# Layer 0 of a hybrid decoder step with the second chunk of tokens reversed, and one product per HGRN level

## Chip, cores and metric

One NeuronCore of a Trainium2 chip runs the whole step. The metric is device time in microseconds (us) of one execution. Engines are named as the profile names them: PE (TensorE, the matrix multiplier), PEld (its weight loads), DVE (VectorE), ACT (ScalarE), POOL (GpSimd) and SP (the queue that issues the weight DMAs).

## The reference, cut to what matters

The program takes 256 prompt tokens and 8 sample tokens (264 columns) through two trunk layers. Layer 0 projects the tokens once and feeds two groups of heads in parallel: 4 retention heads of width 256 and 8 HGRN2 heads of width 128. The change concerns the HGRN2 heads, and the retention heads where they share the order of the tokens:

```python
def _hgrn2(q, k, v, log_f, s0):          # k = 1 - f, with f the forget gate
    def step(s, inp):
        qc, kc, vc, gc = inp
        b = jnp.cumsum(gc, axis=1)
        o_cross = jnp.einsum('bihd,bhdv->bihv', qc * jnp.exp(b), s)
        rel = jnp.exp(jnp.where(causal, b[:, :, None] - b[:, None, :], -jnp.inf))
        att = jnp.einsum('bihd,bjhd,bijhd->bhij', qc, kc, rel)
        o = o_cross + jnp.einsum('bhij,bjhv->bihv', att, vc)
        ...
# retention: the same, with one fixed decay per head
# then: out projection, residual add, a SwiGLU FFN, layer 1 (S5), a second FFN, a final norm
```

So the score of query i and key j is a sum over 128 channels, where each channel has its own decay: the product of the forget gates from j to i.

## The kernel before, in words

**Storage.** Activations lie feature-major: 128 features on the partitions, 264 tokens along the free axis (0 to 255 the prompt, 256 to 263 the samples).

**The stream.** All large products run as one stream of units (`Step.stream`, L104 to L143). A unit is 8 blocks of 128x128 weights. ACT rounds the weights to a high part `whi` (`split`, L85 to L96, the copy on L89), DVE subtracts for the low part `wlo` (L96; POOL does it for every eighth unit). PE then makes three products per block with 264 columns: high by high (L128), high weights by the low activations (L129), low weights by high (L131). `ahead` keeps four units split ahead, so the split of a later unit is emitted at the start of the present one; `flush` emits what was put off in `S.later`, right behind that split.

**Work of the heads.** After each unit `slot` lets the generators in `S.active` go one step. In layer 0 that is `mixers`: in each call it advances the sample generator (`hg_sample` or `ret_sample`: the recurrent states of the 8 sample tokens), then the tails of finished heads, then one of the heads in work (two HGRN heads in turn, or one retention head). The order of each engine's instructions is the order in which these lines are emitted; no scheduler moves them.

**An HGRN head** (`hg_head`, L453). Tokens form two chunks of 128. Inside a chunk a causal pair (i, j) is found at the level l of the highest bit in which the two positions differ: j lies in the left half of a block of 2^(l+1) tokens and i in the right half. For l = 0 to 6 the head does one step:

- PE multiplies, for each chunk j, all 128 keys by the 64 queries that stand in right halves (L496, fp32, two products of 64 columns);
- `decay(l + 1)` on DVE multiplies the left keys `hk` by the decay of the right half (L470) and the right queries `hq` by that of the left half (L471), and forms the next level's decays `pw` (L474);
- DVE copies the wanted scores from PSUM into `score` under a mask (L499).

Then come the product of chunk 1's queries with chunk 0's keys (L505, one product of 128 columns), the products with v (L512 to L515) and the tail.

**A retention head** (`ret_head`, L347): transposes (L355, L358), scores `p` (L360, L362), the decay mask `am` in two DVE products (L370, L371), the products with v (L376, L377), and a tail.

**Samples.** `hg_sample` rescales the states on ACT (L434), adds the outer products on DVE (L435), four states a step, and reads them on PE (L442). `ret_sample` does the same with L319, L322 and L327. `qz` (L280) holds the sample queries, `se` and `so` carry the result out (L285, L290, L293). `hg_sample` waits for the entry "qs", which the head sets in its first step.

**Leaving the layer.** `out_first` (L764) adds the residual column block by block; the RMS norm's sum is closed by the product of L225.

Of the kernel before, what the change touches and what calls it, by code (L numbers as in the profile page):

```python
# [28 lines left out]
C_MASK, C_KDEC, C_W = 0, 7 * 64, 7 * 64 + 8  # L29
# [211 lines left out]
def layer0(S, I, O):  # L241
# [105 lines left out]
    def ret_head(h, H):  # L347
        dec = S.st("pd", 1, w=256)
# [20 lines left out]
        am = S.st("am", 1, w=512)  # L369
        V.tensor_mul(am[:, :256], p[:, :256], dec)  # L370
        V.tensor_mul(am[:, 256:384], p[:, 256:384], dec[:, :128])  # L371
# [83 lines left out]
    def hg_head(h, H):  # L455
# [4 lines left out]
        halves = lambda x, l: x[:, :NP].rearrange("p (b t s) -> p b t s", t=2, s=1 << l)  # L460
        sc = score[h % 2]
        pw = S.st("pw", 2, w=256)
        P = {0: f[:, :NP]}

        def decay(l):

            Pv = P[l - 1].rearrange("p (b t) -> p b t", t=2)
            bc = lambda t: Pv[:, :, t:t + 1].to_broadcast([128, NP >> l, 1 << (l - 1)])
# [5 lines left out]
            V.tensor_mul(P[l], Pv[:, :, 0], Pv[:, :, 1])  # L474
# [11 lines left out]
        vt = S.st("vt", 2, w=256)  # L486
        acopy(vt, pvv[:, :256])
        yield
        at = 256
        for l in range(8):  # L490
            if l in (2, 6):
                pa, at = S.pt("a", 2), 0
            if l < 7:
                for j in range(2):
                    sl = slice(128 * j, 128 * j + 128)
                    PE.matmul(pa[:, at + 64 * j:at + 64 * j + 64], k[:, sl],  # L496
                              q[:, sl].rearrange("p (b t s) -> p b t s", t=2, s=1 << l)[:, :, 1, :], start=True, stop=True)
                decay(l + 1)
                V.copy_predicated(sc.rearrange("p j (b t s) -> p j b t s", t=2, s=1 << l)[:, :, :, 1, :],  # L499
                                  mask[:, C_MASK + 64 * l:C_MASK + 64 * l + 64].rearrange(  # L500
                                      "p (o b s) -> p o b s", o=1, s=1 << l).to_broadcast([128, 2, 64 >> l, 1 << l]),
# [217 lines left out]
    def mixers():  # L719
# [1039 lines left out]
def host(inputs):  # L1759
# [4 lines left out]
    xT = np.concatenate([xp, xs], 0).T[perm]  # L1764
# [16 lines left out]
    for l in range(7):  # L1781
        right = t[t >> l & 1 == 1]
        c[:, C_MASK + 64 * l:C_MASK + 64 * l + 64] = (t[:, None] >> l == (right[None] >> l) - 1)
    lg = np.log((1.0 - 2.0 ** (-5.0 - np.arange(RH))).astype(np.float32)).astype(np.float32).astype(np.float64)
    for h in range(RH):
        for j in range(2):
            c[:, C_KDEC + 2 * h + j] = np.exp((255 - 128 * j - t) * lg[h]) / 16
    A["cst"] = c
    i, j = np.arange(256)[None], t[:, None]
    A["rdec"] = np.stack([np.where(i >= j, np.exp((i - j) * lg[h]) / 16, 0.0) for h in range(RH)]).astype(np.float32)  # L1790
    inv = (10000.0 ** (-(t.astype(np.float32) / np.float32(128)).astype(np.float64))).astype(np.float32)
    pos = np.concatenate([np.arange(256), np.full(8, 2048)]).astype(np.float32)
# [49 lines left out]
```

## Time and profile before

| | us |
|---|---|
| device time, median of 3 runs | 2398.79 (2398.37 to 2399.08) |
| the profiled execution, device time | 2398.75 |
| the profiled execution, span on the core | 2396.9 |
| PE busy in the span | 2358.3 |
| DVE busy | 1600.3 |
| ACT busy | 1115.9 |
| POOL busy | 267.3 |
| mean granted TensorE clock | 0.996 |

The span runs from the first to the last instruction; 1.85 us of the device time lie around it. Layer 0's projection and heads take the span from 0 to about 480 us, the out projection follows to about 570, then come the first FFN, the S5 layer and the second FFN. An engine's busy time is an average over all of this. In the timeline a row gives start, length, engine, line, operation, tiles and the number of merged instructions. Ends of matmuls are modelled, so what a PE instruction costs is read from the starts of its neighbours. An fp32 product shows as two PE records, one for each pass over the weights.

### The profile page before, as it was taken

Reading aid. Unit: us, or ns where it says so; the run is one execution under the profiler, and the core shown is the slowest. Engines: PE = TensorE matmul, PEld = TensorE weight load, DVE = VectorE, ACT = ScalarE, POOL = GpSimd, SP = SyncE. Lnnn points to the kernel's source line nnn. Section 1 sums busy time; section 2 is a strip of 40 time slices with the busy share of each in tenths; the row PEclk is TensorE's granted clock in tenths of the full one; section 3 lists DMA queues with packets and bytes.
Section 4 is the critical chain, followed back from the end, with each engine's and each line's share of the span. In section 5 each row is a group of like instructions: output and inputs, shape, how many; then the busy total and the mean of one; then the engine's idle time right before and its main releaser. Section 6 shows DMA issues by size and latency. Waiting matters only on the chain.

```text
span 2396.9 us, 49380 instructions
## 1 busy us (share of the span) xinstructions
PE 2358.3 (98%) x20331; PEld 2324.7 (97%) x20331; DVE 1600.3 (67%) x2567; ACT 1115.9 (47%) x1612; POOL 267.3 (11%) x363
## 2 busy tenths in 40 slices
PE   8999999999999999999999989999999999999997
PEld 8999999999999999999999969999999999999997
DVE  6777777777877778877756685555555555555555
ACT  6464645554444344444444465454443344434444
POOL 3121111221020111012011140001000000000000
PEclk9999999999999999999999999999999999999999
DMA  7757566765557767777676885556556555565554
GB/s 240 244 201 246 207 234 220 245 209 189 184 195 225 231 218 235 225 224 229 218 239 181 311 316 185 176 186 207 179 182 180 184 184 180 183 182 180 183 165 136
DMA packets 189553, 499.58 MB, mean 208 GB/s; under 512 B 19408, under 2 KB 72128, under 8 KB 188816
## 3 DMA queue, kind: packets, MB, share of 16 engines
q1 hardware_dynamic: 176368, 452.83, 58.2%
q0 software_dynamic: 12960, 43.59, 5.5%
q8 instruction: 160, 2.62, 0.4%
q14 instruction: 65, 0.53, 0.1%
HBM read 452.44 MB, written 43.91 MB: 207 GB/s over the span
## 4 chain that ended last, share of the span: by engine, by line
PE 91%; DVE 3%; ACT 2%; DMA 2%; issue 1%; SPq 0%; DVEq 0%; ACTq 0%
PE acc L128 28%; PE acc L129 28%; PE acc L131 28%; ACT whi L89 1%; PE pa L496 1%; DVE wlo L96 1%; PE pt L1039 1%; DMA raw<-w_in 1%; DVE st L435 0%; DMA a2l<-wb 0%; DMA whi<-wb 0%; PE pt L1024 0%; PE ps L327 0%; PE pt L386 0%; PE pa L131 0%
## 5 line engine op out<-in xcount | busy, mean ns | idle before, releaser
L96 DVE TENSOR_TENSOR wlo<-raw,whi 128x1024 fp32r<-128x1024 f32 (+1 forms) x743 | 898.9, 1213 | 486.6 <-ACT whi L89 473.8
L89 ACT ACTIVATE whi<-raw 128x1024 fp32r<-128x1024 f32 (+1 forms) x767 | 794.0, 1040 | 840.7 <-PE acc L129 558.0
L128 PE MATMUL acc<-xh,whi 128*128 128x264 f32 x3776 | 1086.6, 288 | 7.4 <-ACT whi L650 7.4
L131 PE MATMUL acc<-xh,wlo 128*128 128x264 f32 x3776 | 1071.4, 284 | 0.0
L129 PE MATMUL acc<-xl,whi 128*128 128x264 f32 x3776 | 1070.3, 283 | 0.0
L128 PEld LDWEIGHTS acc<-xh,whi 128*128 128x128 f32 x3776 | 712.3, 189 | 10.9 <-ACT whi L650 7.7
L129 PEld LDWEIGHTS acc<-xl,whi 128*128 128x128 f32 x3776 | 713.3, 189 | 0.4
L131 PEld LDWEIGHTS acc<-xh,wlo 128*128 128x128 f32 x3776 | 709.2, 188 | 0.6 <-POOL wlo L651 0.6
L128 PE MATMUL acc<-a2h,whi 128*128 128x264 f32 x2080 | 594.3, 286 | 0.0
L131 PE MATMUL acc<-a2h,wlo 128*128 128x264 f32 x2080 | 590.0, 284 | 0.0
L129 PE MATMUL acc<-a2l,whi 128*128 128x264 f32 x2080 | 589.6, 283 | 0.0
L128 PEld LDWEIGHTS acc<-a2h,whi 128*128 128x128 f32 x2080 | 392.3, 189 | 1.8 <-issue 1.6
L129 PEld LDWEIGHTS acc<-a2l,whi 128*128 128x128 f32 x2080 | 392.5, 189 | 0.0
L131 PEld LDWEIGHTS acc<-a2h,wlo 128*128 128x128 f32 x2080 | 390.5, 188 | 0.1
L1754 POOL TENSOR_TENSOR xh<-xh,R 128x528 f32<-128x528 f32 x2 | 2.9, 1467 | 725.7 <-DVE R L189 725.7
L96 POOL TENSOR_TENSOR wlo<-raw,whi 128x1024 fp32r<-128x1024 f32 x24 | 58.1, 2423 | 155.0 <-ACT whi L89 141.6
L1589 DVE TENSOR_TENSOR x<-x,acc 128x264 f32<-128x264 f32 x96 | 41.1, 429 | 50.2 <-PE acc L131 49.9
L1577 DVE TENSOR_TENSOR up<-acc,R 128x264 f32<-128x264 f32 x88 | 38.0, 432 | 44.6 <-PE acc L131 44.1
L1570 DVE TENSOR_TENSOR pre<-acc,R 128x264 f32<-128x264 f32 x88 | 38.0, 432 | 41.5 <-PE acc L131 41.0
L1013 POOL DMA_DIRECT2D bc<-s5t x16 | 9.2, 575 | 385.5 <-ACT whi L89 142.5
L220 ACT ACTIVATE sq<-x 128x264 f32<-128x264 f32 x58 | 24.2, 417 | 54.1 <-DVE x L1589 54.1
L322 DVE SCALAR_TENSOR_TENSOR st<-vb,x,st 128x256 f32<-128x256 f32 x64 | 41.3, 710 | 6.5 <-ACT st L319 5.8
(480 smaller groups left out, 1803.6 us busy)
## 6 DMA issues: line engine op xcount, KB each, us to landing
raw<-w_gu SPq DMA_DIRECT2D x352, 512.0 KB
raw<-w_dn SPq DMA_DIRECT2D x128, 512.0 KB
raw<-w_in SPq DMA_DIRECT2D x127, 512.0 KB
raw<-w_glu SPq DMA_DIRECT2D x64, 512.0 KB
raw<-w_dn SPq DMA_DIRECT2D x64, 384.0 KB
raw<-w_out SPq DMA_DIRECT2D x32, 512.0 KB
st<-sret POOLq DMA_DIRECT2D x16, 512.0 KB, 7.6
o_sret<-st POOLq DMA_DIRECT2D x16, 512.0 KB, 6.4
```

Source lines behind the costliest of these rows:

```text
L89: self.nc.scalar.activation(u.hi, u.raw, AF.Copy)
L96: e.tensor_sub(u.lo, u.raw, u.hi.bitcast(F32))
L128: mm(k.acc, u.hi[:, j], h, start=k.done == 0, stop=False)
L129: mm(k.acc, u.hi[:, j], l, start=False, stop=False)
L131: mm(k.acc, u.lo[:, j], h, start=False, stop=k.done == k.total)
L220: self.nc.scalar.activation(sq, self.x[:, kt], AF.Square)
L322: V.scalar_tensor_tensor(stc[:, g], vb[:, :, s], k[:, NP + s:NP + s + 1], stc[:, g], op0=OP.mult, op1=OP.add)
L496: PE.matmul(pa[:, at + 64 * j:at + 64 * j + 64], k[:, sl], q[:, sl].rearrange("p (b t s) -> p b t s", t=2, s=1 << l)[:, :, 1, :], start=Tr ...
L1039: PE.transpose(p[:, 128 * q:128 * q + 128], W[:, i, q].rearrange("p j c -> p (j c)"), S.ident)
L1570: V.tensor_mul(t, acc, R)
L1577: V.tensor_mul(t, acc, R)
L1589: V.tensor_add(S.x[:, nt], S.x[:, nt], acc)
```

## The change

It does the following.

- **Token order.** The host writes the prompt's second chunk in reversed order (`ORDER`) into the input, the rotary tables and the decay tables. `out_first` puts the tokens back: it adds three pieces, the middle one read backwards.
- **One product per level.** With the second chunk reversed, its left keys stand where the first chunk has its right keys. `lefts(l)` copies the left keys of both chunks into one tile `lk` of 128 columns, interleaved, on ACT; the copy goes into `S.later`, so it is emitted behind the next split. One product of `lk` with the 128 right queries of both chunks takes the place of two with 64. The mask keeps, for each query, the keys of its own chunk.
- **Decays and masks** use the same element counts with one more dimension, since left and right are swapped in the second chunk.
- **Retention.** The decay table has 384 columns instead of 256, and the mask `am` is one DVE product instead of two.
- **Order in a unit.** `mixers` advances the tails and the head first, and the sample generator last.

```diff
+ORDER = np.r_[0:128, 255:127:-1, 256:264]
...
 def ret_head(h, H):
-        dec = S.st("pd", 1, w=256)
+        dec = S.st("pd", 1, w=384)
...
-        V.tensor_mul(am[:, :256], p[:, :256], dec)
-        V.tensor_mul(am[:, 256:384], p[:, 256:384], dec[:, :128])
+        V.tensor_mul(am[:, :384], p[:, :384], dec)
...
 def hg_head(h, H):
+        def side(x, l, right):
+            n = 1 << l
+            return bass.AP(tensor=x.tensor, offset=x.offset + n * right,
+                           ap=[list(x.ap[0]), [128 + (-n if right else n), 2], [2 * n, 64 >> l], [1, n]])
         def decay(l):
-            kv, qv = halves(k, l - 1), halves(q, l - 1)
-            V.tensor_mul(kv[:, :, 0, :], kv[:, :, 0, :], bc(1))
-            V.tensor_mul(qv[:, :, 1, :], qv[:, :, 1, :], bc(0))
+            for x, right in ((k, 0), (q, 1)):
+                v = side(x, l - 1, right)
+                V.tensor_mul(v, v, bc(1 - right))
...
+        def lefts(l):
+            t = S.st("lk", 2, w=128)
+            S.later.append(lambda: acopy(t.rearrange("p (b t s) -> p t b s", t=2, s=1 << l), side(k, l, 0)))
+            return t
...
         vt = S.st("vt", 2, w=256)
+        lk = lefts(0)
         acopy(vt, pvv[:, :256])
...
-                for j in range(2):
-                    sl = slice(128 * j, 128 * j + 128)
-                    PE.matmul(pa[:, at + 64 * j:at + 64 * j + 64], k[:, sl],
-                              q[:, sl].rearrange("p (b t s) -> p b t s", t=2, s=1 << l)[:, :, 1, :], start=True, stop=True)
+                PE.matmul(pa[:, at:at + 128].rearrange("p (j b s) -> p j b s", j=2, s=1 << l), lk, side(q, l, 1),
+                          start=True, stop=True)
                 decay(l + 1)
+                if l < 6:
+                    lk = lefts(l + 1)
...
 def mixers():
         while todo or mains or tails or samp or samples:
-            if samp is None and samples:
-                samp = samples.pop(0)
-            if samp is not None and next(samp, "end") == "end":
-                samp = None
-            state["samp"] = samp is not None or samples
...
+            if samp is None and samples:
+                samp = samples.pop(0)
+            if samp is not None and next(samp, "end") == "end":
+                samp = None
+            state["samp"] = samp is not None or samples
             yield
...
 def out_first(nt, g, ss):
-            V.tensor_add(S.x[:, nt], xin.pop(nt), acc)
+            xr = xin.pop(nt)
+            V.tensor_add(S.x[:, nt, :128], xr[:, :128], acc[:, :128])
+            V.tensor_add(S.x[:, nt, 128:NP], xr[:, 255:127:-1], acc[:, 255:127:-1])
+            V.tensor_add(S.x[:, nt, NP:], xr[:, NP:], acc[:, NP:])
```

Three places show how the order moves. Line numbers of the changed kernel differ a little: its splits are L91 and L98, its products of the stream L130, L131 and L133.

The first place is ACT in the first pair of heads, from the activation of the second head's queries on. Before:

```order
L178 ACTIVATE hq<-pre 128x264
L447 ACTIVATE vt<-pt 128x256
L89 ACTIVATE whi<-raw 128x1024
L434 ACTIVATE st<-st,hf 128x128 x4
L89 ACTIVATE whi<-raw 128x1024
L178 ACTIVATE hg<-pre 128x264
L434 ACTIVATE st<-st,hf 128x128 x4
```

And in the changed kernel:

```order
L180 ACTIVATE hq<-pre 128x264
L447 ACTIVATE vt<-pt 128x256
L435 ACTIVATE st<-st,hf 128x128 x4
L91 ACTIVATE whi<-raw 128x1024
L448 ACTIVATE lk<-hk 128x2x64
L435 ACTIVATE st<-st,hf 128x128 x4
L91 ACTIVATE whi<-raw 128x1024
L180 ACTIVATE hg<-pre 128x264
L91 ACTIVATE whi<-raw 128x1024
L448 ACTIVATE lk<-hk 128x2x32x2
```

The rescaling of the sample states has moved ahead of a split, and a copy of left keys stands behind a split in each unit that has a level.

The second place is DVE at the start of the second pair, from the first head's queries to its first level. Before:

```order
L484 TENSOR_TENSOR hq<-hq,hf 128x256
L96 TENSOR_TENSOR wlo<-raw,whi 128x1024
L280 COPY qz<-hq 128x4 x2
L435 SCALAR_TENSOR_TENSOR st<-vb,hk,st 128x128 x4
L189 SCALAR_TENSOR_TENSOR rs<-lnt,rs 128x264
L264 TENSOR_TENSOR x<-x,rs 128x264
L582 TENSOR_TENSOR pre<-acc,R 128x264
L435 SCALAR_TENSOR_TENSOR st<-vb,hk,st 128x128 x4
L267 TENSOR_TENSOR a2l<-x,a2h 128x264
L264 TENSOR_TENSOR x<-x,rs 128x264
L470 TENSOR_TENSOR hk<-hk,hf 128x128
```

And in the changed kernel:

```order
L504 TENSOR_TENSOR hq<-hq,hf 128x256
L282 COPY qz<-hq 128x4 x2
L436 SCALAR_TENSOR_TENSOR st<-vb,hk,st 128x128 x4
L98 TENSOR_TENSOR wlo<-raw,whi 128x1024
L191 SCALAR_TENSOR_TENSOR rs<-lnt,rs 128x264
L266 TENSOR_TENSOR x<-x,rs 128x264
L436 SCALAR_TENSOR_TENSOR st<-vb,hk,st 128x128 x4
L604 TENSOR_TENSOR pre<-acc,R 128x264
L269 TENSOR_TENSOR a2l<-x,a2h 128x264
L266 TENSOR_TENSOR x<-x,rs 128x264
L484 TENSOR_TENSOR hk<-hk,hf 128x2x64
```

Both groups of state updates have moved forward by one row; the same instructions stand ahead of the first decay.

The third place is PE in the last retention head. Before:

```order
L537 MATMUL pt<-sqh,ones_84 128x264
L376 MATMUL po<-am,x 128x256
L377 MATMUL po<-am,x 128x128
L376 MATMUL po<-am,x 128x256
L377 MATMUL po<-am,x 128x128
L128 MATMUL pa<-a2h,whi 128x264
```

And in the changed kernel:

```order
L559 MATMUL pt<-sqh,ones_84 128x264
L377 MATMUL po<-am,x 128x256
L378 MATMUL po<-am,x 128x128
L377 MATMUL po<-am,x 128x256
L378 MATMUL po<-am,x 128x128
L329 MATMUL ps<-st,qz 32x256 x16
L130 MATMUL pa<-a2h,whi 128x264
```

The read of the sample states, which stood 24 products of the stream further on, has moved up by that unit; so have the reads of all 12 heads.

## Rows read from the trace of the kernel before

**Rows 1.** Stretch 183 to 230: busy us of PE, PEld, DVE, ACT, POOL; clock, DMA share, GB/s.

```profile
183.00:230.00 47.00, 47.00 (x405) 46.66 (x404) 33.46 (x95) 19.97 (x31) 9.61 (x11) 1.00 0.71 242
```

**Rows 2.** Groups of PE, 56 to 470 us: busy, mean ns, idle before.

```profile
L496 PE MATMUL pa<-hq,hk 128*128 128x64 f32 x224 | 31.9, 264 | 1.4 <-DVE score L499 1.4
```

**Rows 3.** Timeline of PE, a level 0: queries in steps of two.

```profile
171.12 0.28 PE L131 MATMUL acc<-xh,wlo 128*128 128x264 f32 x1
171.24 0.55 PE L496 MATMUL pa<-hq,hk 128*128 128x64 f32 x4
171.60 0.37 PE L128 MATMUL acc<-xh,whi 128*128 128x264 f32 x1
```

**Rows 4.** Timeline of PE, one fp32 product of 128 columns.

```profile
451.26 0.28 PE L131 MATMUL acc<-xh,wlo 128*128 128x264 f32 x1
451.38 0.38 PE L505 MATMUL pa<-hq,hk 128*128 128x128 f32 x2
451.52 0.37 PE L128 MATMUL acc<-xh,whi 128*128 128x264 f32 x1
```

**Rows 5.** Timeline of PE, before and behind a level 6: queries side by side.

```profile
454.39 0.28 PE L131 MATMUL acc<-xh,wlo 128*128 128x264 f32 x1
...
454.87 0.37 PE L128 MATMUL acc<-xh,whi 128*128 128x264 f32 x1
```

**Rows 6.** Timeline of ACT, DVE and PE from one level of a head to its next.

```profile
196.43 1.06 ACT L89 ACTIVATE whi<-raw 128x1024 fp32r<-128x1024 f32 x1 [2.30 <-PE acc L129]
...
196.95 0.29 DVE L470 TENSOR_TENSOR hk<-hk,pw 128x128 f32<-128x128 f32 x1 [1.45 <-PE pa L496]
...
203.08 0.56 PE L496 MATMUL pa<-hq,hk 128*128 128x64 f32 x4
```

**Rows 7.** Groups of ACT and DVE: busy, mean ns of one, idle before.

```profile
L285 ACT ACTIVATE se<-ps 128x128 f32<-128x128 f32 x8 | 2.1, 268 | 12.4 <-PE ps L442 12.4
...
L764 DVE TENSOR_TENSOR x<-hv,acc 128x264 f32<-128x264 f32 x12 | 5.1, 427 | 11.7 <-PE acc L131 11.7
```

**Rows 8.** Timeline of the second pair's start: ACT, then DVE, then PE.

```profile
173.82 0.41 ACT L178 ACTIVATE hg<-pre 128x264 f32<-128x264 f32 x1
178.71 1.04 ACT L89 ACTIVATE whi<-raw 128x1024 fp32r<-128x1024 f32 x1
...
170.15 1.55 DVE L435 SCALAR_TENSOR_TENSOR st<-vb,hk,st 128x128 f32<-128x128 f32 x4
...
174.55 3.11 DVE L435 SCALAR_TENSOR_TENSOR st<-vb,hk,st 128x128 f32<-128x128 f32 x4 [1.71 <-ACT st L434]
178.27 0.29 DVE L470 TENSOR_TENSOR hk<-hk,hf 128x128 f32<-128x128 f32 x1
...
175.04 0.38 PE L481 MATMUL pt<-ident,hv 128*128 128x128 f32 x2
179.38 0.66 PE L496 MATMUL pa<-hq,hk 128*128 128x64 f32 x4 [0.47 <-DVE score L499]
```

**Rows 9.** Timeline of the last retention head: DVE, then PE.

```profile
474.60 2.47 DVE L322 SCALAR_TENSOR_TENSOR st<-vb,x,st 128x256 f32<-128x256 f32 x4
477.05 1.23 DVE L96 TENSOR_TENSOR wlo<-raw,whi 128x1024 fp32r<-128x1024 f32 x1
478.19 0.39 DVE L280 COPY qz<-x 128x4 f32<-128x4 f32 x4
...
475.21 0.59 PE L376 MATMUL po<-am,x 128*128 128x256 f32 x2
475.64 0.38 PE L377 MATMUL po<-am,x 128*128 128x128 f32 x2
476.30 0.38 PE L377 MATMUL po<-am,x 128*128 128x128 f32 x2
```

**Rows 10.** Timeline of the norm behind layer 0: DVE, then PE.

```profile
570.93 0.43 DVE L221 TENSOR_TENSOR ssx<-ssx,sq 128x264 f32<-128x264 f32 x1
...
572.21 0.61 PE L225 MATMUL pt<-ssx,onesD 128*128 128x264 f32 x2
```

More of the change, by code (lines that the diff above doesn't have):

```diff
@@ L27 @@
 KPERM = [0, 1, 2, 3, 4, 5, 8, 9, 10, 11, 12, 13, 14, 15, 6, 7]
-C_MASK, C_KDEC, C_W = 0, 7 * 64, 7 * 64 + 8
+C_MASK, C_KDEC, C_W = 0, 256, 264
+ORDER = np.r_[0:128, 255:127:-1, 256:264]
 P_G0, P_GF0, P_G1, P_GF1, P_GFIN, P_RGN, P_HGN, P_LB, P_W = 0, 16, 32, 48, 64, 80, 88, 96, 120
@@ L368, in ret_head @@
                          scale=cst[:, C_KDEC + 2 * h + j:C_KDEC + 2 * h + j + 1])
-        am = S.st("am", 1, w=512)
-        V.tensor_mul(am[:, :256], p[:, :256], dec)
-        V.tensor_mul(am[:, 256:384], p[:, 256:384], dec[:, :128])
+        am = S.st("am", 1, w=384)
+        V.tensor_mul(am[:, :384], p[:, :384], dec)
         yield
@@ L493, in hg_head @@
             if l < 7:
-                for j in range(2):
-                    sl = slice(128 * j, 128 * j + 128)
-                    PE.matmul(pa[:, at + 64 * j:at + 64 * j + 64], k[:, sl],
-                              q[:, sl].rearrange("p (b t s) -> p b t s", t=2, s=1 << l)[:, :, 1, :], start=True, stop=True)
+                PE.matmul(pa[:, at:at + 128].rearrange("p (j b s) -> p j b s", j=2, s=1 << l), lk, side(q, l, 1),
+                          start=True, stop=True)
                 decay(l + 1)
-                V.copy_predicated(sc.rearrange("p j (b t s) -> p j b t s", t=2, s=1 << l)[:, :, :, 1, :],
-                                  mask[:, C_MASK + 64 * l:C_MASK + 64 * l + 64].rearrange(
-                                      "p (o b s) -> p o b s", o=1, s=1 << l).to_broadcast([128, 2, 64 >> l, 1 << l]),
+                if l < 6:
+                    lk = lefts(l + 1)
+                m = C_MASK + 256 - (256 >> l)
+                V.copy_predicated(side(flat, l, 1),
+                                  mask[:, m:m + (128 >> l)].rearrange("p (j b o) -> p j b o", j=2, o=1).to_broadcast(
+                                      [128, 2, 64 >> l, 1 << l]),
                                   pa[:, at:at + 128].rearrange("p (j b s) -> p j b s", j=2, s=1 << l))
@@ L1763, in host @@
     xp, xs = f("x_prompt")[0], f("x_sample")[:, 0]
-    xT = np.concatenate([xp, xs], 0).T[perm]
+    xT = np.concatenate([xp, xs], 0)[ORDER].T[perm]
     A["xT"] = np.ascontiguousarray(xT.reshape(KT, 128, T).transpose(1, 0, 2))
@@ L1781, in host @@
     for l in range(7):
-        right = t[t >> l & 1 == 1]
-        c[:, C_MASK + 64 * l:C_MASK + 64 * l + 64] = (t[:, None] >> l == (right[None] >> l) - 1)
+        m, b = C_MASK + 256 - (256 >> l), np.arange(64 >> l)
+        for j in range(2):
+            c[:, m + (64 >> l) * j:m + (64 >> l) * (j + 1)] = t[:, None] >> l == 2 * b + j
     lg = np.log((1.0 - 2.0 ** (-5.0 - np.arange(RH))).astype(np.float32)).astype(np.float32).astype(np.float64)
@@ L1786, in host @@
         for j in range(2):
-            c[:, C_KDEC + 2 * h + j] = np.exp((255 - 128 * j - t) * lg[h]) / 16
+            c[:, C_KDEC + 2 * h + j] = np.exp((t if j else 255 - t) * lg[h]) / 16
     A["cst"] = c
     i, j = np.arange(256)[None], t[:, None]
-    A["rdec"] = np.stack([np.where(i >= j, np.exp((i - j) * lg[h]) / 16, 0.0) for h in range(RH)]).astype(np.float32)
+    dist = np.concatenate([ORDER[None, :NP] - j, j - t[None]], 1)
+    A["rdec"] = np.stack([np.where(dist >= 0, np.exp(dist * lg[h]) / 16, 0.0) for h in range(RH)]).astype(np.float32)
     inv = (10000.0 ** (-(t.astype(np.float32) / np.float32(128)).astype(np.float64))).astype(np.float32)
-    pos = np.concatenate([np.arange(256), np.full(8, 2048)]).astype(np.float32)
+    pos = np.concatenate([np.arange(256), np.full(8, 2048)])[ORDER].astype(np.float32)
     ang = (inv[:, None] * pos[None]).astype(np.float32).astype(np.float64)
```

13 lines of the change are left out of this document (9 added, 4 removed).

## The prediction

> **What bounds the kernel now.** I read the busy shares by stretch first. [...] Then PE's groups: the level products wait for another engine 1.4 us in all [rows 2], three waits of about 0.5 us, of which one is shown [rows 8]. The forecast therefore has two parts: what PE no longer does, and which of the now later partners make it wait.
>
> **The products.** I read a cost from starts, since a matmul's end is modelled. From the last product of the stream ahead of a level to the first behind it 0.48 us pass with two products of 64 columns [rows 3]; with one fp32 product of 128 columns in the same place 0.26 us [rows 4]. The difference, 0.22 us, is one product. So an fp32 product of 64 columns costs as much as one of 128; the columns do not set the price at this size. They do above it: a product of 256 takes 475.64 - 475.21 = 0.43 us [rows 9].
> There are 8 heads with 7 levels, 56 products less (112 products, two records each, are the 224 of [rows 2]): 56 x 0.22 = **12.3 us less** on PE.
> [...]
> One thing no row shows: 128 queries read in steps. At level 0 every second query is read, and at 64 columns that costs what queries side by side cost, 0.48 us [rows 3, 5]. But the stream of 64 columns could be half as fast and still fit under 0.22 us. Bounds: no cost, or 0.22 us more for the 8 level 0 products, 1.8 us. I take none, since level 0 and level 6 agree, and keep 1.8 for the range.
>
> **The copies of left keys.** 56 copies on ACT; the nearest row is a copy of 128x128 at 0.27 us [rows 7], so 15 us of ACT. At most 14 of them fall in the stretch of 47 us, 3.8 us on top of 20.0 [rows 1]: ACT still has half its time. Each stands behind a split and blocks what follows on ACT until DVE has decayed the keys. In the row shown DVE decays them by 197.24 and the split ends at 197.49 [rows 6], so the copy ends near 197.8. The head's next product comes at 203.08: 5.3 us to spare. DVE even starts that decay earlier, since PE no longer reads these keys itself and the row's wait of 1.45 us for PE falls to the queries' product, one instruction later. Cost in the steady part: none.
> It is different at the start of the pairs two to four. There DVE is late: the first decay ends at 178.56, and PE has already waited 0.47 us at 179.38, so it stood ready at 178.91 [rows 8]; one product less puts that at 178.7. If DVE comes as late as now, the copy goes behind the split that ends at 179.75 and is done near 180.0: a wait of 1.3 us in place of 0.47, three times, 2.5 us more. But the change also moves the rescaling of the sample states ahead of a split (1.04 us) and an activation (0.41) on ACT, for which DVE waited 1.71 us [rows 8]; if all of that reaches DVE, the present waits vanish, 1.4 us less. Between -1.4 and +2.5 I take the middle, **+0.5 us**.
>
> **The samples' reads.** All 12 move up by one unit, DVE's updates by less. In the steady part DVE has slack. Two places are close. At the start of a pair the read now follows the transposes of 175.04, so PE arrives near 175.2. DVE now ends the second four updates at 177.66 [rows 8]. They start when ACT has rescaled, which moves up by 1.45 us: from 173.10 on, and at the 1.55 us that the first four take they end at 174.65; at the 3.11 us that these took now, at 176.2. I take no wait, since the rows before show four in 1.55 and the 3.11 have a hole; the bound is 2.5 us (updates as late as now), at three such places 7.5, the rival below.
> In the last retention head the read follows the second product of line 377 at once, near 476.5 [rows 9]. DVE ends its updates at 477.07, then a small copy and the queries' copies (0.39); the split of 1.23 us now stands behind them instead of ahead, so they end at 478.58 - 1.23 = 477.35. A wait of **+0.8 us**; bounds 0 and 2.
>
> **What stays beside other work.** The mask of the retention scores becomes one operation instead of two, a little less DVE. Each residual add becomes three: two of 128 columns at the 0.29 of a product of that size [rows 6] and a small one under that, at most 0.45 us more than 0.43 [rows 7], 16 times; before that line DVE waited 11.7 us for PE [rows 7], which covers it. The last add counts most: behind it the sum of squares ends at 571.36 and PE asks for it at 572.21 [rows 10]; 0.45 us later is still in time, and so it is if reading backwards doubles one piece (0.29 more). The retention's larger decay table is 64 KB more in 4 transfers, at a DMA share of 0.71 [rows 1], issued on POOL in the same place: no cost; uncovered, 256 KB at 242 GB/s would be 1.1 us. Decays and masked copies keep their element counts; a row of the added dimension does not exist, and DVE's spare 13.5 us of 47 [rows 1] covers even 0.1 us on each.
>
> **Sum**, against the profiled execution's 2398.75 us, which is within 0.04 of the median: 2398.75 - 12.3 + 0.5 + 0.8 = **2387.7 us**. Everything behind layer 0 only starts earlier.
>
> **Rivals.**
> *No gain from merging.* The 64-column products cost 0.22 us because of how the queries are read, and with 128 columns the price doubles. For it: both fit [rows 3]. Against it: level 6, whose queries lie side by side, costs the same [rows 5], and the 128 columns of [rows 4] pay 0.22. Time: 2398.75 + 0.5 + 0.8 = 2400.0. [...] Chance 4%.
> *Late sample reads.* PE waits 2.5 us at three starts, and more where DVE is late: 7.5 to 11 us back, 2395 to 2399. For it: DVE is already the late one there, in a row with a hole of over 1 us [rows 8]. Against: its wait for ACT goes. Chance 6%.
> *Slower: the copies come late.* ACT is strictly in order: a late decay holds the copy, the copy holds the split. From turn to turn of a head lie two units, 48 products at 0.12 us [rows 4] and two levels at 0.36: 6.5 us. It decides once DVE ends a decay more than 5.2 us after the product of that turn, since split and copy take 1.3. At the start of a pair it is so: the product starts at 171.24 [rows 3], the decay ends at 178.56 [rows 8], 7.3 us; with split and copy 8.6, a wait of 2.1. Eight further levels of the 56 like that bring 16.8 us: 2404.5. Against it: DVE's time to spare in [rows 1]. Chance 3%.
>
> **Numbers.** My forecast has 87%. Its range: up by 1.8 (steps), 2.0 (copies at their bound) and 1.2 (last read at its bound), 2392.7; down by 1.9 and 0.8, 2385.0. About 0.2%, 4.8 us, can be told from no change: below 2394.0 counts as faster, above 2403.6 as slower. Faster 87%, same 10%, slower 3%.
>
> **What would show it.** PE's groups should have 112 records of 128 columns with `lk` in place of 224, and 0.26 us from product to product around them; PE's waits on ACT copies and DVE at the three starts should stay under 2 us in all; one wait near 0.8 us before the read in the last retention head. Wrong would be 0.48 us around a level, waits of PE for `lk` in the middle of a pair, or waits before the samples' reads at each start.

## The result, and the profile after

The changed kernel takes **2387.05 us** (median of 4 runs, 2386.86 to 2387.64), the kernel before 2398.93 (2398.37 to 2400.79) beside it: a ratio of 0.995, 95% interval 0.9932 to 0.9967. The forecast was 2387.7. The profiled execution of the changed kernel took 2387.64 us with a span of 2385.9; the one before had 2396.9. So 11.0 us have to be found between the two traces.

Ahead of the change's rows a note on the lines: those of the changed kernel are higher (the split is now L91, its low half L98, the stream L130 to L133, the level product L515, the decay L484, the copy of left keys `lk` L448).

The stretch of [rows 1], in the middle of the second pair, in the changed kernel (busy us of PE, PEld, DVE, ACT, POOL; clock, DMA share, GB/s):

```profile
183.00:230.00 47.00, 47.00 (x403) 46.68 (x402) 38.08 (x96) 22.69 (x39) 9.73 (x11) 1.00 0.75 255
```

PE is busy for all of the 47 us at a granted clock of 1.00 in both kernels, so what it spends on the heads adds to the end, and the other engines count only where PE waits for them. ACT has 2.7 us more (8 instructions more). DVE has 4.6 us more, mostly because eight updates of a retention head's sample states (line 324, 5.8 us) fall into this stretch only here. What bounds the stage has not changed. The group of the level products, 56 to 470 us, against [rows 2]:

```profile
L515 PE MATMUL pa<-hq,lk 128*128 128x128 f32 x112 | 21.9, 276 | 1.2 <-ACT lk L448 1.2
```

112 records of 128 columns stand where 224 of 64 stood, and one lasts 276 ns against 264. The timeline of PE around a level 0, whose queries are read in steps of two as in [rows 3]:

```profile
63.34 0.28 PE L133 MATMUL acc<-xh,wlo 128*128 128x264 f32 x1
63.46 0.39 PE L515 MATMUL pa<-hq,lk 128*128 128x128 f32 x2
63.60 0.37 PE L130 MATMUL acc<-xh,whi 128*128 128x264 f32 x1
```

From the last product of the stream to the next one 0.26 us pass (63.60 - 63.34), where 0.48 passed. Both kernels issue the stream in the same order, so one can ask in both traces when the same product starts. The first one starts at 5.54 us before and at 5.32 in the changed kernel. Counted from there, the changed kernel is ahead by 0.5 us just ahead of the first level (at 55 us), by 3.3, 6.0 and 8.7 where pairs two, three and four begin (167, 280 and 393), by 12.35 behind the last level (456), by 10.6 at 500 us and by 10.8 at 2290. The product at 500 us, first before, then in the changed kernel (503.73 - 492.87 = 10.86, less the 0.22 of the first product):

```profile
503.73 0.28 PE L128 MATMUL pa<-a2h,whi 128*128 128x264 f32 x1
...
492.87 0.28 PE L130 MATMUL pa<-a2h,whi 128*128 128x264 f32 x1
```

So the four pairs of HGRN heads give 11.8 us, the last retention head takes 1.7 back, and 0.9 us lie elsewhere: 0.2 at the first product, 0.5 between it and the first level, 0.2 behind 1000 us, where the change alters no work of PE. The kernels of the experiments do the same work ahead of the first level, and there they are 0.0 to 0.5 us ahead of the kernel before, in no order that their edits explain. So I take the 0.9 us for chance.

The waits of PE in the HGRN and retention heads (total, times, longest), 56 to 600 us; before there were only the three of 0.5 us in [rows 2]:

```profile
PE pa L515 <- ACT lk L448: 1.2, 2, 0.6
PE pt L546 <- ACT x L366: 0.7, 1, 0.7
PE pt L292 <- DVE lnth L189: 0.5, 1, 0.5
```

Two waits of 0.6 for a copy of left keys lie at the starts of pairs two and three. The other two lie in the last retention head. A wait makes the later products late by more than its idle time: 0.85 us for each of the first two, 1.7 us for the two in the last head (0.95 of it behind line 546). The parts can be read from kernels of the experiments that differ in one of them. The new order alone, in the kernel before, gains 1.4 us in the pairs (the three old waits are gone, and the first pair loses 0.4) and loses 1.7 in the last head. The kernel with the residual add in one piece has the rest of the change too and no wait at the starts; against the new order alone its pairs gain 12.1 us. So the balance is 12.1 + 1.4 - 1.7 (starts) - 1.7 (last head) = 10.1 us in the heads, and with the 0.9 us of chance 11.0.

### The profile page after: what moved, and what is told of

The parts are those of the page before. It is cut to its first block, busy times and chain, and to the rows that moved or that the text cites. A ratio compares the mean times of both kernels' runs of the same rounds, so it can differ in the third digit from the quotient of the medians.

```text
span 2385.9 us, 49285 instructions
## 1 busy us (share of the span) xinstructions
PE 2348.4 (98%) x20219; PEld 2314.9 (97%) x20219; DVE 1607.7 (67%) x2595; ACT 1129.1 (47%) x1668; POOL 271.8 (11%) x363
## 4 chain that ended last, share of the span: by engine, by line
PE 78%; DVE 1%; ACT 1%; issue 0%; DMA 0%; DVEq 0%; ACTq 0%
PE acc L130 25%; PE acc L131 25%; PE acc L133 25%; PE pt L1357 1%; PE pt L1064 1%; PE pt L1049 0%; ACT a2h L1458 0%; PE pa L133 0%; DMA wcs<-wc 0%; PE pa L130 0%; PE pa L131 0%; DVE xh L1779 0%; PE pt L1573 0%; PE pt L1715 0%; DVE wlo L98 0%
## 5 line engine op out<-in xcount | busy, mean ns | idle before, releaser
L98 DVE TENSOR_TENSOR wlo<-raw,whi 128x1024 fp32r<-128x1024 f32 (+1 forms) x743 | 898.5, 1212 | 487.7 <-ACT whi L91 479.7
L91 ACT ACTIVATE whi<-raw 128x1024 fp32r<-128x1024 f32 (+1 forms) x767 | 794.5, 1040 | 821.2 <-PE acc L131 534.7
L130 PE MATMUL acc<-xh,whi 128*128 128x264 f32 x3776 | 1086.9, 288 | 6.9 <-ACT whi L672 6.9
L133 PE MATMUL acc<-xh,wlo 128*128 128x264 f32 x3776 | 1071.2, 284 | 0.0
L131 PE MATMUL acc<-xl,whi 128*128 128x264 f32 x3776 | 1070.0, 283 | 0.0
L130 PEld LDWEIGHTS acc<-xh,whi 128*128 128x128 f32 x3776 | 712.2, 189 | 13.3 <-ACT whi L672 7.2
L131 PEld LDWEIGHTS acc<-xl,whi 128*128 128x128 f32 x3776 | 713.0, 189 | 0.4
L133 PEld LDWEIGHTS acc<-xh,wlo 128*128 128x128 f32 x3776 | 709.0, 188 | 0.6 <-POOL wlo L673 0.6
L130 PE MATMUL acc<-a2h,whi 128*128 128x264 f32 x2080 | 594.8, 286 | 1.2 <-ACT whi L91 1.2
L133 PE MATMUL acc<-a2h,wlo 128*128 128x264 f32 x2080 | 590.5, 284 | 1.7 <-POOL wlo L98 1.7
L131 PE MATMUL acc<-a2l,whi 128*128 128x264 f32 x2080 | 590.1, 284 | 0.0
L130 PEld LDWEIGHTS acc<-a2h,whi 128*128 128x128 f32 x2080 | 392.8, 189 | 3.1 <-ACT whi L91 1.9
L131 PEld LDWEIGHTS acc<-a2l,whi 128*128 128x128 f32 x2080 | 393.0, 189 | 0.0
L133 PEld LDWEIGHTS acc<-a2h,wlo 128*128 128x128 f32 x2080 | 391.0, 188 | 2.0 <-POOL wlo L98 2.0
L98 POOL TENSOR_TENSOR wlo<-raw,whi 128x1024 fp32r<-128x1024 f32 x24 | 60.3, 2518 | 151.4 <-ACT whi L91 137.1
```

What stands on the lines that cost most here:

```text
L91: self.nc.scalar.activation(u.hi, u.raw, AF.Copy)
L98: e.tensor_sub(u.lo, u.raw, u.hi.bitcast(F32))
L130: mm(k.acc, u.hi[:, j], h, start=k.done == 0, stop=False)
L131: mm(k.acc, u.hi[:, j], l, start=False, stop=False)
L133: mm(k.acc, u.lo[:, j], h, start=False, stop=k.done == k.total)
```

## The experiments

Beside these runs the kernel before took 2398.5 to 2398.6 us, that is 0.3 to 0.4 us less than beside the changed kernel; the changed kernel's 2387.05 was not taken again, so differences of this size from it say nothing. The experiments go by question.

### Is it the columns, the copies, or the order?

**Two products of 64 again**, from the copied keys, all else as changed:

```diff
-                PE.matmul(pa[:, at:at + 128]..., lk, side(q, l, 1), start=True, stop=True)
+                for j in range(2):
+                    PE.matmul(pa[:, at + 64 * j:at + 64 * j + 64]..., lk, side(q, l, 1)[:, j], start=True, stop=True)
```

> The changed kernel with its single level product taken apart again: two fp32 products of 64 columns each from the same copied left keys. Order, copies, reversed tokens and all else stay. Theory (an fp32 product costs about 0.22 us at 64 and at 128 columns alike, and PE is the bound): 56 x 0.22 = 12.3 us slower than the changed kernel, near 2399.4 us, and 0.48 us from the last product of the stream ahead of a level to the first behind it instead of 0.26. Rival (the gain of 11.9 us came from the order in the unit, from the shorter masks or from the keys no longer held by PE): within 3 us of the changed kernel.

Measured: 2398.3 us (2397.49 to 2399.92), ratio to before 0.9999 (0.9991 to 1.0008). Its group of products:

```profile
L516 PE MATMUL pa<-hq,lk 128*128 128x64 f32 x224 | 31.1, 261 | 0.0
```

The whole gain goes when the halves are multiplied apart: 2398.3 - 2387.05 = 11.25 us, 0.20 a level. It is 1.1 us less than expected; this kernel's trace has no wait at the starts, which cost the changed kernel's 1.7. Copies, stepped reads, the reversed chunk and the new order together are worth nothing measurable.

**The samples' step first again**, in the changed kernel (the five lines that step `samp` go back to the top of the loop in `mixers`):

> The changed kernel with the sample generator moved back to the front of each unit; the single product and the copies stay. Theory (the order decides only which of a few waits PE has): the waits in the last retention head (1.2 us in the profile of the changed kernel) go, the copies at the starts of pairs two to four come about 1.3 us late each instead of 0.6 twice; 2386 to 2390 us. Rival (without the head first, the copies come late at many levels): 2 us or more per start, over 2393 us.

Measured: 2388.41 us (2388.15 to 2388.49), 1.4 more than the changed kernel. The waits of PE in the heads are now three, and those of the last head are gone:

```profile
PE pa L515 <- ACT lk L448: 4.0, 3, 1.3
```

**The new order alone**, in the kernel before (the same five lines moved to the end of the loop):

> The kernel before with the new order in the unit alone (heads before samples), two products of 64 columns and no copies. Theory (the order alone trades waits of about 1.5 us for others of about 1.5 us): 2397 to 2400.5 us. Rival (the order carries part of the 11.9 us): 2396 or less.

Measured: 2398.4 us (2398.11 to 2401.02), ratio 1.0001 (0.9992 to 1.001). The three old waits of 0.5 were gone from its trace and the two of 0.7 and 0.5 in the last head had come. So the order alone trades one for the other. It pays in the changed kernel, because without it the starts would cost 1.3 each.

### Do stepped reads or the added pieces cost anything?

**Queries side by side at every level** (the first 128 columns are always read, so the scores are not the reference's):

```diff
-                PE.matmul(pa[:, at:at + 128]..., lk, side(q, l, 1), start=True, stop=True)
+                PE.matmul(pa[:, at:at + 128], lk, q[:, :128], start=True, stop=True)
```

> The changed kernel with every level product reading the 128 queries of the first chunk side by side instead of the right queries of both chunks in steps (the scores are then not those of the reference: the step in reading is what is left out). Theory (reading in steps costs nothing at 128 columns): within 1 us of 2387. Rival (steps of two at level 0 cost up to 0.22 us a product): 1.8 us faster; if all steps cost, up to 10 us faster.

Measured: 2386.45 us (2386.25 to 2386.79). Its level 0 takes 0.26 too:

```profile
63.71 0.28 PE L133 MATMUL acc<-xh,wlo 128*128 128x264 f32 x1
...
63.97 0.37 PE L130 MATMUL acc<-xh,whi 128*128 128x264 f32 x1
```

Over the whole first pair, 14 levels, its products stay at the same distance from those of the changed kernel (0.21 to 0.24 us, from 50 to 170 us, counted from the first product). Steps of two fp32 values cost nothing here. Its median is 0.6 us lower; its trace lacks the two waits at the starts, 0.85 each, which would explain more than that. They are the subject of the section after the next.

**The residual add in one piece** (nothing is turned back, so the second chunk of the residual is mixed up):

```diff
-            V.tensor_add(S.x[:, nt, :128], xr[:, :128], acc[:, :128])
-            V.tensor_add(S.x[:, nt, 128:NP], xr[:, 255:127:-1], acc[:, 255:127:-1])
-            V.tensor_add(S.x[:, nt, NP:], xr[:, NP:], acc[:, NP:])
+            V.tensor_add(S.x[:, nt], xr, acc)
```

> The changed kernel with the residual add of the out projection in one piece as before, without turning the second chunk round (this leaves out the un-reversing, so the second chunk of prompt tokens is mixed up from there on; the time of the rest does not depend on the values). Theory (the three adds are covered by DVE's waiting for PE): within 0.5 us of the changed kernel. Rival (reading backwards is slow, or the last add delays the norm): over 1 us faster.

Measured: 2386.6 us (2386.21 to 2386.73). From 480 to 580 us, where the adds are, its products keep their distance from the changed kernel's within 0.02 us. The two pieces more cost nothing; again the two waits at the starts are missing from its trace.

### How much time do the copies have?

**Each copy three times** (the same values):

```diff
-            S.later.append(lambda: acopy(t.rearrange(...), side(k, l, 0)))
+            S.later.append(lambda: [acopy(t.rearrange(...), side(k, l, 0)) for _ in range(3)])
```

> The changed kernel, with each left-key copy done three times in a row (the same values). Theory of the prediction (ScalarE has 5.3 us to spare around each level of the steady part, so 0.4 to 0.6 us more per level is hidden there; only at the two or three starts does the product wait up to 0.6 us longer): 2387 to 2389. Rival (the spare time is not really free, since a later split is a later low half and a later product): 56 x 0.4 = 22 us more at most; over 2392 would decide for it.

Measured: 2387.54 us (2387.26 to 2390.93), 0.5 us more for 112 copies more. PE waits for `lk` only at starts (2.0 us in two places). The spare time of the prediction is real.

**The copy one unit later**:

```diff
-            S.later.append(lambda: acopy(...))
+            S.later.append(lambda: S.later.append(lambda: acopy(...)))
```

> The changed kernel with each copy emitted one unit (about 3.2 us) later, behind the split of the unit after. Theory (5.3 us to spare in the steady part, none at the starts of pairs two to four): no wait in the steady part, 1.3 to 3.4 us more at each of three starts, 2391 to 2397 us. Rival (the spare time of the steady part is not there, since ACT is strictly in order): waits at most of the 56 levels, over 2410 us.

Measured: 2405.51 us (2405.22 to 2408.6), ratio 1.0033 (1.002 to 1.0045): far above the 2391 to 2397 that I had expected. The waits of PE in the heads, and the timeline of PE at the start of the second pair:

```profile
PE pa L515 <- ACT lk L448: 13.0, 4, 3.6
```

```profile
173.97 0.79 PE L515 MATMUL pa<-hq,lk 128*128 128x128 f32 x2 [3.61 <-ACT lk L448]
174.42 0.57 PE L130 MATMUL acc<-xh,whi 128*128 128x264 f32 x1
174.79 0.42 PE L131 MATMUL acc<-xl,whi 128*128 128x264 f32 x1
175.01 0.42 PE L133 MATMUL acc<-xh,wlo 128*128 128x264 f32 x1
...
176.77 0.36 PE L131 MATMUL acc<-xl,whi 128*128 128x264 f32 x1
176.96 0.28 PE L133 MATMUL acc<-xh,wlo 128*128 128x264 f32 x1
```

All 13.0 us are four waits, one at the first level 0 of each pair (2.1, then 3 x 3.6); the other 52 levels stand a whole unit of delay without any wait. And a wait of 3.6 costs more than itself: behind it the products come every 0.22 us instead of 0.12 until 176.8. The stretches around this wait show the clock (the column before the last two is the granted one):

```profile
168.00:174.00 6.00, 2.39 (x21) 2.19 (x19) 5.18 (x13) 3.75 (x9) 0.20 (x1) 0.96 0.31 106
174.00:180.00 6.00, 6.00 (x49) 5.64 (x50) 5.58 (x10) 1.99 (x4) 4.47 (x4) 0.76 0.27 63
```

After PE had stood idle for 3.6 us, the granted clock was 0.76 over the next 6 us. In the changed kernel the same two stretches, with a wait of 0.6, were granted 1.00. Going by the same product in both traces, each of the three waits makes PE 4.1 us late, and until the products come at their old pace another 1.1, 2.3 and 1.3 us are lost. The steady part was expected rightly. The starts were not: three of them make PE 4.1 us late instead of 1.3 to 3.4, the first pair has a wait too, and the clock was left out.

**The copy at once**, ahead of the next split instead of behind it:

```diff
-            S.later.append(lambda: acopy(...))
+            acopy(...)
```

> The changed kernel with each copy of left keys emitted at once in the head's step, ahead of the next split instead of behind it. Theory (ACT has time, and splits are done units ahead, so a split that waits for a decay costs nothing; the copies at the starts of pairs come sooner by a split of 1.04 us): the two waits of 0.6 us go, 2385.5 to 2387 us. Rival (the place behind the split is what keeps PE fed): splits come late, over 2390 us.

Measured: 2398.34 us (2394.75 to 2399.44): the whole gain is lost. I had expected a little less time than the changed kernel's. Since the profiled execution was the fastest of 11, I ran it again for a second trace:

> The kernel with all copies at once, a second time, for its trace: its median was 2398.3 while its profiled execution took 2394.75. In that one ScalarE stood 65 us (changed kernel: 16 us) waiting for decays at the head of its queue, and samples' reads and key transposes waited 6 us for ScalarE and VectorE. Theory (these late reads are what it costs, and they vary with the transfers): median within 2397 to 2399 again, and an execution near 2398 shows some 3.5 us more in the same waits. Rival (a cost that no wait shows, in the products' stream itself): the waits stay near 6 us at 2398.

Measured: 2397.98 us (2396.23 to 2400.08), the profiled one 2396.49. The waits of ACT for the decays, 56 to 500 us, first in the changed kernel and then here:

```profile
ACT lk L448 <- DVE hk L484: 16.4, 17, 1.6
```

```profile
ACT lk L448 <- DVE hk L484: 63.7, 31, 3.2
```

The waits of PE in the heads (the last head's two and one of 0.4 are left out):

```profile
PE pt L537 <- DVE hk L528: 3.8, 4, 1.5
PE pt L357 <- ACT sph L448: 3.7, 3, 1.3
```

and one place of each, first ACT, then DVE, then PE:

```profile
349.61 0.42 ACT L180 ACTIVATE x<-pre 128x264 f32<-128x264 f32 x1 [4.94 <-DVE pre L604]
349.94 0.26 ACT L448 ACTIVATE sph<-pt 128x128 f32<-128x128 f32 x1
...
345.32 0.29 DVE L528 TENSOR_SCALAR hk<-hk,pw 128x128 f32<-128x128 f32 x1
...
348.01 1.23 DVE L98 TENSOR_TENSOR wlo<-raw,whi 128x1024 fp32r<-128x1024 f32 x1
349.14 0.44 DVE L604 TENSOR_TENSOR pre<-acc,R 128x264 f32<-128x264 f32 x1
...
345.67 0.44 PE L537 MATMUL pt<-ident,hk 128*128 128x128 f32 x2 [1.24 <-DVE hk L528]
350.26 0.66 PE L357 MATMUL pt<-ident,x 128*128 128x128 f32 x4 [1.24 <-ACT sph L448]
```

The level products are in time, as expected (no wait for `lk` at all), but DVE falls behind: the last decay of a head (L528) and the projections it has to hand over (L604) come late, and ACT's copy `sph`, which frees a PSUM buffer for the transposes of line 357, stands behind that. Going by the same product, these two waits make PE 6.7 us late in the first trace (2.3 and 3.0 us of idle time) and 8.9 in the second (3.8 and 3.7); a wait at the first start adds 0.8, and the changed kernel's 1.7 at the starts are not there. That is 5.8 of the 7.1 and 8.0 of the 8.9 us by which the two profiled executions are over the changed kernel's. The two were 1.7 us apart, so these waits vary from execution to execution; whether with the transfers, as the theory had it, no trace shows. The medians are another 3.6 and 1.5 us higher; no execution near 2398 was traced, and this stays open.

What makes DVE late is not isolated either. The copy waits for its decay at the head of ACT's queue, and the split that feeds DVE's next low half waits behind it; that is one candidate. The record shows a second one at the place above. Ahead of those rows a decay of DVE had taken 2.48 us instead of 0.28, beside a low half on POOL:

```profile
335.95 2.81 POOL L98 TENSOR_TENSOR wlo<-raw,whi 128x1024 fp32r<-128x1024 f32 x1 [7.77 <-ACT whi L91]
...
336.42 2.48 DVE L484 TENSOR_TENSOR hk<-hk,pw 128x128 f32<-128x128 f32 x1
```

In the changed kernel this low half (331.67) meets no instruction that is held up. The second trace of the copies at once shows the like near the last levels of pair four: beside the low half on POOL at 451.16 (3.18 us), line 488 takes 2.37 us at 451.99, against 0.15 in the changed kernel (331.02). No run separates the two candidates; the next section has more on the second.

### What makes the starts late?

Three kernels were meant to save what the changed kernel still loses. **Retention samples ahead of the heads, HGRN samples behind them**:

```diff
+            if samp is None and samples and samples[0][0] == "ret":
+                samp = samples.pop(0)
+            if samp is not None and samp[0] == "ret" and next(samp[1], "end") == "end":
+                samp = None
...
-            if samp is not None and next(samp, "end") == "end":
+            if samp is not None and samp[0] == "hg" and next(samp[1], "end") == "end":
```

> The changed kernel with the retention samples moved back ahead of the heads and the HGRN samples left behind them. Theory (the two waits in the last retention head, 0.72 and 0.54 us, come from the retention samples' rescaling and updates standing in front): they go, 1.2 to 1.9 us less, 2385 to 2386 us. Rival (they come from PE being early there): same as the changed kernel.

Measured: 2392.78 us (2392.21 to 2393.35): 5.7 more than the changed kernel, which neither the theory nor the rival allows. Its waits in the heads:

```profile
PE pa L515 <- ACT lk L448: 3.5, 3, 1.2
PE pt L537 <- DVE hk L528: 1.1, 4, 0.3
PE pt L546 <- ACT x L366: 0.9, 1, 0.9
PE pt L292 <- ACT w L390: 0.7, 1, 0.7
```

All three starts wait, the last decays are late, and the last head did not improve. The mixture is worse than either order. At a start the copy of level 0 stands on ACT behind the rescaling of the samples' states (1.27 us) and a split (1.04), and is done 1.2 us late. That suggested the next one.

**Level 0's copy at once**, the others behind the split:

```diff
-            S.later.append(lambda: acopy(...))
+            copy = lambda: acopy(...)
+            copy() if l == 0 else S.later.append(copy)
```

> The changed kernel, but the copy of level 0's left keys is issued at once, ahead of the next split; the copies of levels 1 to 6 stay behind it. Level 0's keys need no decay, so this copy has nothing to wait for on VectorE. Theory (at the starts of pairs the level-0 product waits for a copy that is ready to run and stands behind one state update of 1.27 us and one split of 1.05 us on ScalarE): the 0.85 us at each of two starts goes, 1.7 us in all, and no sample's read waits newly: 2384.9 to 2385.9. Rival (any copy ahead of a split costs, as when all copies were issued at once, which took 2398.3): 7 of the 56 copies... here 8 of 56 are ahead, so 11.3 x 8/56 = 1.6 us more: 2388.7 or later.

Measured: 2386.95 us (2386.62 to 2387.53), 0.1 less than the changed kernel and between the theory and the rival. The waits for `lk` at the starts were gone from its trace, but 0.8 us were lost anew at the start of the first pair, where the read of the HGRN samples (line 443) came too early for DVE's state updates. And **the same with the samples' step first**:

> The same with the samples' step put back ahead of the heads' step in each unit. Theory: samples first cost three waits of 1.3 us for level 0's copy (4.0 us against 1.2 us) and saved the 1.2 us of waits in the last retention head, for 2388.4; with the copy at once the three waits go, so 2388.4 - 4.0 = 2384.4, within 0.8 us. Rival (the three waits come back on another copy, the decay's, as before the change with its 0.5 us each): 2386 or later.

Measured: 2389.53 us (2389.17 to 2390.03), a miss for the theory and as the rival had it, and this settled the matter. The three waits stayed, at 1.6:

```profile
PE pa L516 <- ACT lk L448: 4.7, 3, 1.6
```

So they were not waits for level 0's copy, and the product that waits says so: in the changed kernel it is the level 1 of the pair's first head, whose keys DVE has to decay first. The rows of the changed kernel at the second pair's start, POOL, then DVE, then ACT, then PE:

```profile
171.36 2.64 POOL L98 TENSOR_TENSOR wlo<-raw,whi 128x1024 fp32r<-128x1024 f32 x1 [20.94 <-ACT whi L91]
...
171.67 2.62 DVE L266 TENSOR_TENSOR x<-x,rs 128x264 f32<-128x264 f32 x1
174.21 0.28 DVE L484 TENSOR_TENSOR hk<-hk,hf 128x128 f32<-128x128 f32 x1
...
174.32 0.43 ACT L267 ACTIVATE a2h<-x 128x264 fp32r<-128x264 f32 x1 [2.47 <-DVE x L266]
174.65 1.04 ACT L91 ACTIVATE whi<-raw 128x1024 fp32r<-128x1024 f32 x1
175.60 0.30 ACT L448 ACTIVATE lk<-hk 128x128 f32<-128x128 f32 x1
...
175.96 0.49 PE L515 MATMUL pa<-hq,lk 128*128 128x128 f32 x2 [0.59 <-ACT lk L448]
```

A product of 264 columns that DVE does in 0.42 us took 2.62; it began 0.3 us behind POOL's low half and ended 0.3 behind it (174.29 against 174.00). POOL makes the low half of every eighth unit, and one of these falls at each start. In the kernel with level 0's copy at once the same moment looks like this:

```profile
172.55 3.60 POOL L98 TENSOR_TENSOR wlo<-raw,whi 128x1024 fp32r<-128x1024 f32 x1 [21.05 <-ACT whi L91]
...
172.83 0.43 DVE L266 TENSOR_TENSOR x<-x,rs 128x264 f32<-128x264 f32 x1
...
174.71 2.52 DVE L98 TENSOR_TENSOR wlo<-raw,whi 128x1024 fp32r<-128x1024 f32 x1 [0.46 <-ACT whi L91]
```

Here the product of 264 came through and DVE's own low half was caught instead (2.52 us against 1.22, and it ended 1.08 behind POOL's); nobody waits for that one at once. POOL's row is longer too, 3.60 us instead of the 2.4 it takes in the kernel before: DVE's instructions ran one behind the other at its beginning, and here POOL seems to have waited for them. The 0.8 us lost anew at the first pair's start are the same thing: there POOL's low half (58.62, for 2.38 us) met the four state updates:

```profile
57.59 3.58 DVE L436 SCALAR_TENSOR_TENSOR st<-vb,hk,st 128x128 f32<-128x128 f32 x4
...
61.22 0.41 PE L443 MATMUL ps<-st,qz 128*32 128x128 f32 x2 [0.41 <-DVE st L436]
```

while in the changed kernel it met a decay (L484, 2.10 us in place of 0.28) for which no product waited. Over the starts that I compared (1st to 3rd are the starts of pairs two to four):

| kernel, start | POOL's low half, us | what DVE did slowly | product's wait, us |
|---|---|---|---|
| before, each of three | 2.38 to 2.39 | four state updates, 3.11 (1.55 undisturbed) | 0.5 |
| changed, 1st and 2nd | 2.64, 2.63 | L266, 2.62 (0.42) | 0.6 |
| changed, 3rd | 3.62 | low half, 2.52 (1.22) | none |
| queries side by side, 1st and 2nd | 3.61, 3.60 | low half, 2.52, 2.51 | none |
| one add, 1st and 2nd | 3.62, 3.61 | low half, 2.52 | none |
| level 0's copy at once, 1st and 2nd | 3.60, 3.62 | low half, 2.52 | none |
| copies three times, 1st | 3.64 | low half, 2.53 | none |
| copies three times, 2nd | 2.64 | L266, 2.63 | 1.3 |
| samples first, each of three | 2.37 to 2.38 | four state updates, 3.11 to 3.12 | 1.3 |
| the same, level 0's copy at once | 2.38 | four state updates, 3.11 to 3.12 | 1.6 |

Beside each of these low halves one instruction of DVE, or one of four updates, takes 1.3 to 2.2 us longer than its kind, and the start depends on which one. The kernel with three copies has both outcomes in one trace, with the copies of level 0 in the same place; so it is the meeting that goes with the wait, and the copy of level 0 at once did not mend the starts by its place. No run takes POOL's low half away from a start; that it is the cause is read from these rows. In each the slow row of DVE ends behind POOL's: line 266 by 0.3 us, a low half by 1.1, the four updates by 1.3.

No version of these beats the changed kernel by more than the measurement can tell: 2386.95 against 2387.05.

## Why the prediction was right

**The products: right, with the price.** The forecast was 56 x 0.22 = 12.3 us less. In traces without a wait at the starts it is 12.1 from the new order alone to the kernel with the rest of the change, and 11.6 from the products taken apart to the merged ones; by the medians, the two products of 64 cost 11.25 us when they were put back. An fp32 product with its own weights takes the same 0.2 us at 64 and at 128 columns: in the kernel before, 0.36 us pass from one product of line 131 to the next where no fp32 product stands between them, 0.59 with one of 128 columns (451.26 to 451.85) and 0.81 with two of 64 (171.12 to 171.93). No run separates the loading of the weights from a fixed price of another kind.

**The stepped queries: right to take none**, and the 1.8 us kept for them fall away: 14 levels in a row kept pace with side-by-side reads within 0.03 us.

**The copies in the steady part: right.** There is no wait for `lk` in the middle of any pair, three copies for one cost at most 0.5 us, and only the four level 0 products noticed a delay of a whole unit. That last run also bears on the third rival, the late copies: its mechanism exists, and it took a unit of delay to bring it about. There were four late levels instead of its eight, but three of them cost 5.2 to 6.4 us instead of 2.1: a wait of 3.6, and the clock, which it did not count.

**The starts of the pairs: within the bounds, wrong in reason.** The forecast was +0.5 between -1.4 and +2.5; in the pairs 1.7 are lost and 1.4 gained, +0.3. The step that failed is the reading of the hole in the four updates of 3.11 us: "I take no wait, since the rows before show four in 1.55 and the 3.11 have a hole". The hole was POOL's low half in the kernel before:

```profile
173.99 2.39 POOL L96 TENSOR_TENSOR wlo<-raw,whi 128x1024 fp32r<-128x1024 f32 x1 [20.08 <-ACT whi L89]
```

It did not go with the earlier rescaling; it moved to another DVE instruction. The sentence "if all of that reaches DVE, the present waits vanish, 1.4 us less" left it out. This row beside [rows 8] would have shown it.

**The samples' reads: right at the starts, and in the last head within the bounds of 0 and 2, but twice the size and not in that place.** No read waits at a start. In the last retention head I expected 0.8 us before the read of line 329; it waits for nothing. There is 0.7 before line 546 and 0.5 before line 292, and by the later products the head loses 1.7 us. The same two waits come with the new order alone, and moving the retention samples back ahead did not remove them; what brings them stays open. The step that failed is the order on DVE behind [rows 9]: I let its updates start where they had started against PE. In the changed kernel they start 1.72 us ahead of the first product of line 377 (461.88 against 463.60), before it was 0.61 ahead (474.60 against 475.21), mostly since PE had been held up before line 546 (0.72 us idle, 0.95 in the later products):

```profile
461.88 2.56 DVE L324 SCALAR_TENSOR_TENSOR st<-vb,x,st 128x256 f32<-128x256 f32 x4
464.39 0.41 DVE L282 COPY qz<-x 128x4 f32<-128x4 f32 x4
...
459.69 0.71 PE L546 MATMUL pt<-vt,kd 128*128 128x128 f32 x4 [0.72 <-ACT x L366]
463.60 0.59 PE L377 MATMUL po<-am,x 128*128 128x256 f32 x2
465.00 1.93 PE L329 MATMUL ps<-st,qz 128*32 128x256 f32 x32
```

The queries' copies end at 464.80, and PE arrives at 465.00. The queries were ready 0.2 us early: the wait further up stands where I had looked for one at the read.

**What stays beside other work: right.** The adds in one piece changed nothing past 480 us.

**Why was the sum off by only 0.65 us?** In part by luck. The sum of the terms was 11.0 us less, and the heads gave 10.1: the products 0.2 less than forecast, the last head 0.9 less, the starts 0.2 more. The 0.9 us by which the changed kernel's profiled execution was ahead outside the heads made up for that, and no term of the forecast stands for them. The median of the changed kernel lies 0.6 below this execution, the slowest of its four; the other three may lack a wait at a start, as other kernels' traces do, but they have no trace.

## What to carry to other kernels

In this kernel an fp32 product that loads its own weights costs the same at 64 columns as at 128 (0.23 us for one of 128, 0.45 for two of 64), so two products of 64 that could share a left side were worth merging, even for a copy on an engine with time to spare. Where a helper's place in an engine's queue is chosen, try it behind the work that others need sooner, even though it then comes later itself: here the copies ahead of the split lost all 11 us (ACT waited 63.7 us for decays in 31 places, in place of 16.4 in 17), the copies behind it none. And when a row of DVE is longer than its kind, look at POOL at that time before explaining it by the order.

## What the runs showed of the hardware

- In the rows of the table, the slow instruction of VectorE beside GpSimd's low half of 128x1024 ended 0.3 to 1.3 us behind it: 0.42 us became 2.62, 1.22 became 2.52, four state updates of 1.55 in all became 3.11. Where VectorE's product of line 266 came through first, GpSimd's row was 3.6 us instead of 2.4. Which instruction it is can differ where the rows look alike (in the kernel with three copies, line 266 starts 0.31 us behind POOL's low half at both starts, comes through at one and is caught at the other), and with it go 0.85 us at a start in the changed kernel: differences of 0.5 us between two versions of this kernel are below that and say nothing of the edit.
- In the kernel with the copy one unit later, a single wait of 3.6 us of TensorE was followed by a granted clock of 0.76 over the next 6 us (products 0.22 us apart instead of 0.12); three such waits cost 1.1, 2.3 and 1.3 us on top of themselves. In the changed kernel, waits of 0.6 left the clock at 1.00.
